# Hybrid encoder trunk: the attention heads run as one two-burst pipeline, and the projection's matmuls are ordered behind each burst

## Chip, cores, metric

One core of a Trainium2 chip. The metric is the device time of one execution in microseconds (us), median of three runs. PE is the matmul engine (TensorE; PEld its weight loads), DVE is VectorE, ACT is ScalarE, POOL is GpSimd, SP issues most DMAs.

## The reference, cut to what matters

Two layers; 512 tokens, width 2048. Per layer:

```python
h = rmsnorm(x, g_pre)
z = h @ w_in                      # one projection, columns split nine ways
log_a = log_sigmoid(ga @ w_alpha + b_alpha) / 16        # GLA decay
o_gla = rmsnorm(gla_chunk_causal(gq, gk, gv, log_a)) * silu(gg)   # 4 heads, state per 64-token chunk
o_att = rmsnorm(chunk_band_attention(aq, ak, av, rel_bias)) * silu(ag)  # 8 heads of 128
y = concat([o_gla, o_att]) @ w_out
x = x + rmsnorm(y, g_post)
```

For one attention head, with the 512 tokens in four tiles `i` of 128: scores of tile `i` against keys 0 to `(i+1)*128`, plus a bias by distance, softmax over the row, times `v`.

## The kernel before, in words

**The projections.** They are fp32-accurate products made of three reduced-format matmuls each: an operand is split into a high part (`wh`, an ACT cast, line 261) and a remainder (`wl`, a DVE subtraction, line 271). Blocks of weights are handled in pairs by a Strassen-like scheme: sums and differences of weight blocks (DVE, lines 255, 257, 278), seven products P1 to P7 with four chunks each. One "job" is one product and chunk. In the pair of query/key blocks (`feature_major`) a job is 24 matmuls of 128x256 (line 463); elsewhere it is 12 matmuls of 128x512 (line 473). Jobs come from one list, `stream`; loads, casts and remainders are made up to three jobs ahead. The buffers of `wh` come round every four jobs and those of `wl` every three, so a cast for a later job waits for the matmuls of an earlier one.

**The side work.** After each job, `pace()` calls `pump(n)`, which advances a generator in `tasks` by `n` steps (2.1 per job in the attention stretch). The generators trace the attention, the decay and the GLA heads in small pieces between the jobs.

**A head** (class `Head`) is made of these steps:

- `scores(i)` (lines 1044 to 1065): three matmuls into one PSUM tile; DVE adds the bias and takes the row extreme (line 1055, a custom operation and a read of its accumulator); ACT takes the exponential (line 1059).
- `trans(i)` (lines 1067 to 1076): the tile's probabilities are transposed on PE (line 1071) and copied out of PSUM by ACT (odd `i`, line 1074) or DVE (even `i`, line 1076).
- `mix(i)` (lines 1078 to 1095): probabilities times `v` on PE (line 1089, fp32: two passes each) into a quarter of one PSUM tile `ps_o`, kept for all four `i`; then ACT squares the quarter and sums it (line 1095, with a read of its accumulator).
- `gate()`: DVE adds up (line 1099), POOL takes the power -1/2 (line 524), DVE scales the four quarters (line 1103).
- `turn()`: four transposes of the gated output (line 1114), ACT out of PSUM (line 1117), a split, DMAs.

All these PSUM tiles come from one pool of four (`aux()`). A PE write into a tile waits until the earlier reads of the same tile are over, other columns included. This shows as waits in the order below.

**What sets the order.** The kernel is traced in program order; a list scheduler with a clock of its own then places each engine's instructions, by priority and readiness, and the engines run their lists strictly in that order. `tc.issue_after(x)` adds an edge: what is traced inside it goes behind `x` on the same engine's list. Before the change, two heads at a time are traced step by step by the string `ORDER`, one step per pump step, and nothing holds a job's matmuls back: the scheduler puts them wherever an attention step isn't ready.

Of the kernel before, what the change touches and what calls it, by code (L numbers as in the profile page):

```python
# [15 lines left out]
P = 128  # L16
L = 2
S = 512
# [18 lines left out]
def hybrid_trunk(  # L37
# [112 lines left out]
    lows, loads, last_turn, first_high = [], [], [None], []  # L150
    last_cast, last_low, last_mm, last_load, last_h, last_copy = [None], [None], [None], [None], [None], [None]
# [242 lines left out]
    def fast_gemm(l, pair, consume, rate=0.0, skip=0, feature_major=False, after=None, end=False, lag=0, ops=A, prod=None, acc=None, steps=False):  # L394
# [84 lines left out]
        def step(k, c):  # L479
            if k == "P2" and (end or gates) and c == 0 or k == "P5" and parted and c == 0 and "Z" not in acc:  # L480
                acc["Z"] = [aux()[:, :wide], aux()[:, :wide]]
            job = take(l, b0, k, c)
            behind = half_turns[1] if (k, c) == ("P4", 3) and half_turns else last_mm[0] if apart4 else None
            with tc.issue_after(behind) if behind else nullcontext():
                matmuls(job, k, c, range(2))
            issued.add((l, b0, k, c))
            ahead()
            if c == 3:
                if k == "P1" and not parted:
                    copies("p1", acc["X"])  # L490
                elif k == "P2" and parted:
                    copies("p2", acc[target[k]])
                elif k == "P5":
                    copies("p5", acc[target[k]])
                elif k == "P6":
                    copies("x", acc["X"])
                else:
                    if k == "P7" and (end or parted or gates):
                        copies("x7", acc["X"])
                    for t in range(2):  # L500
                        finished(k, t)
            if after is not None:
                after(k, c)
            pace()
# [340 lines left out]
    def layer(l):  # L845
# [42 lines left out]
        def forget_gate_decay():  # L888
# [6 lines left out]
            def finish_tile(t, la, lah, lal):  # L895
                if t % 2 == 0:
                    decay.append(slot(f"g{9 + t // 2}", [2, 512]))
                ps_d = aux()
                nc.tensor.matmul(ps_d, later, lah, start=True, stop=False)
                nc.tensor.matmul(ps_d, later, lal, start=False, stop=True)  # L900
# [6 lines left out]
            for t in range(NT):  # L907
                ps_g = aux()
# [9 lines left out]
                yield  # L918
                lah, lal = t2(dtype=F32R), t2(dtype=F32R)
                split(lah, lal, la)  # L920
                yield
                yield
                pend.append((t, la, lah, lal))
                if t:
                    finish_tile(*pend.pop(0))
                    yield
            for _ in range(4):
                yield
# [107 lines left out]
        class Head:  # L1036
# [7 lines left out]
            def scores(self, i):  # L1044
# [6 lines left out]
                nc.tensor.matmul(ps[:, :n], self.ql[:, t], self.kh[:, :n], start=False, stop=True)  # L1051
# [15 lines left out]
            def trans(self, i):  # L1067
                lk = (i + 1) * P
                ps = aux()
                for j in range(i + 1):  # L1070
                    nc.tensor.transpose(ps[:, j * P : (j + 1) * P], self.prob[i][:, j * P : (j + 1) * P], ident)  # L1071
                pt = self.pt[i] = t2((lk,))
                if i % 2:
                    nc.scalar.copy(pt, ps[:, :lk])
                else:
                    nc.vector.tensor_copy(pt, ps[:, :lk])

            def mix(self, i):
# [9 lines left out]
                for j in range(i + 1):  # L1088
                    nc.tensor.matmul(  # L1089
# [3 lines left out]
                    )  # L1093
# [33 lines left out]
        ORDER = (  # L1127
            "aS3 aS2 aS1 aS0 aT3 bS3 aT2 aP3 bS2 aT1 aP2 bS1 aT0 aP1 bS0 aP0 - aG "
            "bT3 bT2 bP3 bT1 bP2 bT0 bP1 bP0 - bG"
        ).split()  # L1130

        def attend(hd, qk):
            heads = {"a": Head(hd, qk, 0), "b": Head(hd + 1, qk, 1)}

            def turn(h):
                h.turn()
                if h.hd % 2:
                    heads_done.add(hd)

            for _ in range(5 if hd == HEADS[0] else 0):  # L1140
                yield
            for step in ORDER:
                if step == "-":
                    yield
                    continue
                h = heads[step[0]]
                if step[1] == "S":
                    h.scores(int(step[2]))
                elif step[1] == "T":
                    h.trans(int(step[2]))  # L1150
                elif step[1] == "P":
                    h.mix(int(step[2]))
                else:
                    h.gate()
                    delayed.append([8, lambda h=h: turn(h)])
                yield
# [4 lines left out]
        def qk_consume(p):  # L1161
            sets = {}

            def f(j, h, b, src, comb):
# [11 lines left out]
                if h and b:  # L1176
                    tasks.append(attend(4 * p + 2 * j, sets[j]))
# [7 lines left out]
        until(lambda: 0 in heads_done)  # L1185
        tasks.insert(0, forget_gate_decay())
# [482 lines left out]
```

## Time and profile before

| what | value |
|---|---|
| runs | 1583.02 us median of 3 (1581.57 to 1583.92) |
| the profiled execution's own time | 1582.65 us |
| its span, first to last instruction | 1580.5 us |
| PE busy | 1570.5 us, 99% |
| DVE busy | 1287.6 us, 81% |
| ACT busy | 928.6 us, 59% |
| attention stretch of layer 1 / layer 2 | about 236 to 490 us / 1024 to 1278 us |

The profiled execution lies 2.15 us over its span and 0.37 us under the median. Each row of a group in the profile gives the line, the engine, the operation, the tiles by name (`ax` is a PSUM tile of the side work, `mm` one of the projections), the shape, a count, and then the busy time, the mean ns of one, and the idle time before it with what ended that. In the timeline a row gives the start, the length from the first start to the last end, and the count of merged instructions.

### The profile page before, as it was taken

The numbers are of one execution on the slowest core, as the hardware profiler recorded it, in microseconds if no ns is written. First come the engines' busy times: TensorE is split into PE (matmuls) and PEld (weight loads), VectorE is DVE, ScalarE is ACT, GpSimd is POOL, SyncE is SP. The second block draws the span as 40 slices with busy tenths as digits, with TensorE's granted clock in tenths as the row PEclk, the third lists the DMA queues.
The fourth block names the chain that finished last, engine by engine and source line by source line (L and its number), as shares of the span: only waits on it lengthen the run. The fifth ranks groups of instructions, "written<-read, shape, count | busy, mean of one in ns | idle before, by whom it ended". The sixth has DMA issues, their size and how long they took to land.

```text
span 1580.5 us, 24991 instructions
## 1 busy us (share of the span) xinstructions
PE 1570.5 (99%) x9054; PEld 1363.2 (86%) x9054; DVE 1287.6 (81%) x1723; ACT 928.6 (59%) x1551; POOL 138.9 (9%) x230
## 2 busy tenths in 40 slices
PE   9999999999999999999999999999999999999998
PEld 7888999998888777888888899999988887788886
DVE  5989968578786978998989878785886878699887
ACT  7655545657555556665786446455674655576644
POOL 0221000001000000100122000001010000001001
PEclk9999999999999999999999999999999999999999
DMA  9888895785859768689879998847969597686987
GB/s 370 264 263 295 306 332 190 229 304 183 312 173 313 271 227 306 241 301 387 304 250 360 368 332 312 307 148 235 332 213 313 175 334 263 233 297 226 343 302 206
DMA packets 137738, 439.40 MB, mean 278 GB/s; under 512 B 15364, under 2 KB 27908, under 8 KB 137584
## 3 DMA queue, kind: packets, MB, share of 16 engines
q1 hardware_dynamic: 118800, 372.65, 67.3%
q0 software_dynamic: 18528, 64.88, 12.1%
q8 instruction: 71, 1.16, 0.3%
q14 instruction: 51, 0.42, 0.1%
q10 hardware_dynamic: 288, 0.30, 0.1%
HBM read 378.20 MB, written 61.62 MB: 278 GB/s over the span
## 4 chain that ended last, share of the span: by engine, by line
PE 94%; DMA 3%; DVE 1%; ACT 1%; issue 0%; POOL 0%; SPq 0%; POOLq 0%; DVEq 0%; ACTq 0%
PE mm L473 54%; PE mm L463 20%; PE ax L473 6%; PE mm L380 4%; PE ax L1089 2%; PE ax L1071 1%; PE ax L1278 1%; PE ax L1248 1%; DMA g<-in_w_ag_dram 1%; DMA A<-sa 1%; PE ax L1051 1%; PE ax L1049 1%; PE ax L1050 1%; DVE wl L271 1%; DMA sa<-S 0%
## 5 line engine op out<-in xcount | busy, mean ns | idle before, releaser
L473 PE MATMUL mm<-wh,sa 128*128 128x512 f32 (+1 forms) x1600 | 502.6, 387 | 0.8 <-DMA sa<-S 0.8
L473 PEld LDWEIGHTS mm<-wh,sa 128*128 128x128 f32 x1600 | 296.9, 188 | 61.6 <-DMA sa<-S 1.2
L261 ACT CAST wh<-raw 128x1024 fp32r<-128x1024 f32 (+2 forms) x233 | 234.3, 1009 | 191.3 <-PE mm L473 69.5
L271 DVE TENSOR_TENSOR wl<-raw,wh 128x1024 fp32r<-128x1024 f32 (+2 forms) x233 | 269.5, 1162 | 75.9 <-PE mm L473 33.7
L261 ACT CAST wh<-H 128x1024 fp32r<-128x1024 f32 (+1 forms) x208 | 211.9, 1021 | 177.9 <-PE mm L473 62.3
L473 PE MATMUL mm<-wl,sa 128*128 128x512 f32 (+1 forms) x800 | 310.1, 388 | 0.4 <-DVE wl L271 0.4
L271 DVE TENSOR_TENSOR wl<-H,wh 128x1024 fp32r<-128x1024 f32 (+1 forms) x208 | 245.0, 1179 | 47.4 <-PE mm L473 18.3
L463 PE MATMUL mm<-sa,wh 128*128 128x256 f32 x1280 | 236.1, 284 | 0.0
L473 PE MATMUL mm<-wh,a 128*128 128x512 f32 (+1 forms) x672 | 215.4, 387 | 0.0
L463 PEld LDWEIGHTS mm<-sa,wh 128*128 128x128 f32 x1280 | 199.8, 191 | 0.5
L463 PE MATMUL mm<-sa,wl 128*128 128x256 f32 x640 | 180.6, 284 | 0.0
L473 PEld LDWEIGHTS mm<-wl,sa 128*128 128x128 f32 x800 | 150.2, 188 | 30.9 <-DVE wl L271 1.6
L473 PEld LDWEIGHTS mm<-wh,a 128*128 128x128 f32 x672 | 124.4, 188 | 24.2
L255 DVE TENSOR_TENSOR H<-H,raw 128x1024 f32<-128x1024 f32 (+1 forms) x120 | 141.0, 1180 | 0.3
L473 PE MATMUL mm<-wl,a 128*128 128x512 f32 (+1 forms) x336 | 130.8, 390 | 0.5 <-DVE wl L271 0.5
L261 ACT CAST wh<-g 128x1024 fp32r<-128x1024 f32 x84 | 81.3, 974 | 76.3 <-DVE g L255 25.7
L463 PEld LDWEIGHTS mm<-sa,wl 128*128 128x128 f32 x640 | 122.1, 191 | 0.2
L473 PE MATMUL mm<-wh,g 128*128 128x512 f32 (+1 forms) x416 | 120.5, 367 | 0.0
L271 DVE TENSOR_TENSOR wl<-g,wh 128x1024 fp32r<-128x1024 f32 x84 | 93.7, 1119 | 16.3 <-PE mm L463 7.4
L463 PE MATMUL mm<-a,wh 128*128 128x256 f32 x512 | 94.9, 285 | 0.0
L524 POOL TENSOR_TENSOR sm<-sm,mhalf 128x2 f32<-128x2 f32 (+2 forms) x40 | 38.9, 973 | 615.7 <-DVE sm L1099 295.7
L421 ACT COPY ev<-mm 128x512 f32<-128x512 f32 (+1 forms) x112 | 64.2, 573 | 45.8 <-PE mm L473 31.2
(284 smaller groups left out, 2493.7 us busy)
## 6 DMA issues: line engine op xcount, KB each, us to landing
raw<-in_w_dram SPq DMA_DIRECT2D x287, 512.0 KB, 5.4
sa<-S SPq DMA_DIRECT2D x176, 512.0 KB, 4.4
sa<-A SPq DMA_DIRECT2D x48, 512.0 KB, 6.0
H<-in_w_dram SPq DMA_DIRECT2D x48, 512.0 KB, 5.1
sa<-oS SPq DMA_DIRECT2D x32, 512.0 KB, 5.8
g<-in_w_dram SPq DMA_DIRECT2D x20, 512.0 KB, 7.0
S<-g POOLq DMA_DIRECT2D x18, 512.0 KB, 7.9
raw<-in_w_ag_dram SPq DMA_DIRECT2D x32, 264.0 KB, 4.5
```

The costliest lines, as they stand in the source:

```text
L255: nc.vector.tensor_tensor(out=h, in0=h, in1=r, op=ALU.add)
L261: last_cast[0] = nc.scalar.copy(self.wh[:, z, :], src[:, z, :]).ins
L271: last_low[0] = nc.vector.tensor_tensor(out=self.wl[:, z, :], in0=self.src[:, z, :], in1=self.wh[:, z, :].bitcast(F32), op=ALU.subtract).ins
L380: nc.tensor.matmul(pss[o], a(part, kk, o) if callable(a) else a[:, part, t], rhs[:, kk, :], start=(i == 0 and kk == 0 and m == 0), stop=(i ...
L421: last_copy[0] = nc.scalar.copy(e, src[t]).ins
L463: nc.tensor.matmul(dst, lhs[:, kk, f], a[:, part, tok], start=(fresh and kk == 0 and m == 0 and ft % 2 == 0), stop=(c == 3 and kk == 1 and ...
L473: last_mm[0] = nc.tensor.matmul(out_ps[t], a[:, part, tok], rhs[:, kk, :], start=(fresh and kk == 0 and m == 0), stop=(c == 3 and kk == 1 ...
L524: nc.gpsimd.tensor_tensor(out=out_r, in0=v, in1=mhalf[:, : v.shape[-1]], op=ALU.pow)
L1049: nc.tensor.matmul(ps[:, :n], self.qh[:, t], self.kh[:, :n], start=True, stop=False)
L1050: nc.tensor.matmul(ps[:, :n], self.qh[:, t], self.kl[:, :n], start=False, stop=False)
L1051: nc.tensor.matmul(ps[:, :n], self.ql[:, t], self.kh[:, :n], start=False, stop=True)
L1089: nc.tensor.matmul(o, self.pt[i][:, j * P : (j + 1) * P], av[hd // 4, j // 2][:, j % 2, (hd % 4) * P : (hd % 4 + 1) * P], start=(j == 0), ...
```

## The change

1. `ORDER` and `attend` go. One generator, `attention()`, runs the eight heads as a pipeline. A head has four quarters: `first` (scores 3 and 2), `second` (transposes of 3 and 2, scores 1 and 0), `third` (mix 3 and 2, transposes of 1 and 0), `fourth` (mix 1 and 0, gate). Each burst traces a quarter of the older head and one of the next head together: `third` of the old with `first` of the new, then `fourth` of the old with `second` of the new. The turn of the head before that stands at the front of a burst. Between bursts it gives 5 to 7 pump steps to the jobs. After six heads the pipeline is emptied and the decay runs; then the last two heads.
2. Scores 1 and 0 now share one PSUM tile (`last_scores`: columns 0:256 and 256:512), as do the transposes of 1 and 0, which take one ACT copy in place of one ACT and one DVE copy.
3. `last_att` remembers the last matmul traced of the side work (scores, mix, the decay's second product). In the four pairs QK01, QK45, GK and GV0 each job's matmuls are traced inside `issue_after(last_att[0])`.
4. In `forget_gate_decay` the two products of tile `t-1` are traced right behind the gate product of tile `t`.

```diff
@@ fast_gemm.step
             behind = half_turns[1] if (k, c) == ("P4", 3) and half_turns else last_mm[0] if apart4 else None
+            if b0 in (QK01, QK45, GK, GV0) and last_att[0]:
+                behind = last_att[0]
             with tc.issue_after(behind) if behind else nullcontext():
                 matmuls(job, k, c, range(2))
...
@@ Head
-            def scores(self, i):
+            def scores(self, i, ps=None):
...
-                ps = aux()
+                ps = aux() if ps is None else ps
...
+            def last_scores(self):
+                ps = aux()
+                self.scores(1, ps[:, 0:256])
+                self.scores(0, ps[:, 256:512])
...
+        def attention():
...
+            def second(h):
+                h.trans(3)
+                h.trans(2)
+                h.last_scores()
+            def third(h):
+                h.mix(3)
+                h.mix(2)
+                h.trans(1, 0)
+            def fourth(h):
+                h.mix(1)
+                h.mix(0)
+                h.gate()
...
+            for z in (0, 1, 2, 3, 4, 5, None, "decay", 6, 7, None):
...
+                for n, old, new in ((7 if early else 5, third, first), (7 if early else 6, fourth, second)):
+                    if gated:
+                        turn(gated)
+                        gated = None
+                    if prev:
+                        old(prev)
+                    if h:
+                        new(h)
+                    for _ in range(n):
+                        yield
+                gated, prev = prev, h
```

The count of matmuls is the same before and after. What moves is the order. In the rows below `[waits ...]` names the engines' (or DMA queues') counters for which an instruction waits.

PE's list before, at the place where one head's mix(1) is done (`L1089`, output `ax_4087`, two matmuls; `L1071` is another tile's transpose, `L463` are the jobs' matmuls):

```order
L1071 MATMUL ax_4225<-cst,t_692_3986 128x128 [waits DVE_49]
L463 MATMUL mm_2935<-sa_4023,wh_4066 128x256 [waits DMAHW7_49]
L1089 MATMUL ax_4087<-g_263_1493,t_721_4137 128x128 [waits Activation_49]
L1089 MATMUL ax_4087<-g_263_1493,t_721_4137 128x128
L463 MATMUL mm_2935<-sa_4023,wh_4066 128x256
L463 MATMUL mm_2935<-sa_4023,wl_4120 128x256
L463 MATMUL mm_2935<-sa_4023,wh_4066 128x256 x2
L463 MATMUL mm_2935<-sa_4023,wl_4120 128x256
```

Behind mix(1) stand matmuls of jobs; mix(0) of this head, which writes the same PSUM tile, stands 29 rows further down.

PE's list after, in the burst of layer 1 that does `fourth` of the pipeline's second head and `second` of its third (`L1098` writes `ax_3251`: mix(1), then mix(0), of the older head; `L1080` the transposes of tiles 3 and 2, `L1051` to `L1053` with `ax_3411` scores 1 and then scores 0 of the newer head, `L464` the jobs):

```order
L464 MATMUL mm_2884<-sa_3163,wl_3225 128x256
L1098 MATMUL ax_3251<-g_175_980,t_548_3266 128x128 [waits Activation_49]
L1098 MATMUL ax_3251<-g_175_980,t_548_3266 128x128
L1080 MATMUL ax_3398<-cst,t_550_3275 128x128 [waits PE_49,Activation_49]
L1080 MATMUL ax_3398<-cst,t_550_3275 128x128 x3
L1080 MATMUL ax_3405<-cst,t_553_3283 128x128 [waits Activation_49]
L1080 MATMUL ax_3405<-cst,t_553_3283 128x128 x2
L1051 MATMUL ax_3411<-g_462_2806,g_460_2804 128x256 [waits DVE_49]
L1052 MATMUL ax_3411<-g_463_2807,g_460_2804 128x256
L1053 MATMUL ax_3411<-g_462_2806,g_461_2805 128x256
L1098 MATMUL ax_3251<-g_175_980,t_548_3266 128x128 [waits Activation_49]
L1051 MATMUL ax_3411<-g_462_2806,g_460_2804 128x256 [waits DVE_49]
```

Between mix(1) and mix(0) now stand only the seven transposes and scores 1; mix(0) waits for ACT; scores 0 stands directly behind mix(0) and waits for DVE; the next job's matmuls follow after scores 0.

DVE's list before, around one head's gate (`L1055` the reduction of a score tile, `L1099` the sum that starts the gate, `L1103` the gate's scaling, `L271` the jobs' remainders):

```order
L1055 ISA t_623_3606,sm_3607<-ax_3602,bias_2980 128x128 [waits PE_49]
L1055 ISA sm_3607 128x1
L1062 SCALAR_TENSOR_TENSOR sm_3610<-sm_3296 128x4 [waits Activation_49]
L271 TENSOR_TENSOR wl_3638<-raw_3286,wh_3592 128x1024 [waits PE_49]
L1025 MEMSET bias_3363 64x64 [waits Activation_49]
L1099 TENSOR_TENSOR sm_3683<-sm_3295,sm_3361 128x4 [waits DVE_49,Activation_49]
L271 TENSOR_TENSOR wl_3676<-raw_3594,wh_3641 128x1024 [waits PE_49]
L1103 SCALAR_TENSOR_TENSOR sg_3461<-ax_3460,sm_3684,sg_3461 128x128 [waits Pool_49]
L1103 SCALAR_TENSOR_TENSOR sg_3461<-ax_3460,sm_3684,sg_3461 128x128 x3
```

The head's own score tiles are reduced before `L1099`; no score tile is reduced between it and the scaling.

DVE's list after, at the same burst as the PE rows above (`L1083` copies the transposes of tile 2, `L1108` is the sum that starts the older head's gate, `L1057` reduces score tiles: `t_574` is scores 1 and `t_576` is scores 0 of the newer head, `L1112` the gate's scaling):

```order
L272 TENSOR_TENSOR wl_3376<-raw_3130,wh_3344 128x1024 [waits PE_49]
L1083 COPY t_572_3406<-ax_3405 128x384 [waits PE_49]
L1108 TENSOR_TENSOR sm_3390<-sm_2917,sm_3097 128x4 [waits Activation_49]
L1057 ISA t_574_3415,sm_3416<-ax_3411,bias_2770 128x256 [waits DVE_49,PE_49]
L1057 ISA sm_3416 128x1
L1112 SCALAR_TENSOR_TENSOR sg_3252<-ax_3251,sm_3391,sg_3252 128x128 [waits DMAHW2_49,Pool_49]
L1112 SCALAR_TENSOR_TENSOR sg_3252<-ax_3251,sm_3391,sg_3252 128x128 x3
L1057 ISA t_576_3422,sm_3423<-ax_3411,bias_2770 128x128 [waits DVE_49,PE_49]
L1057 ISA sm_3423 128x1
```

The gate's sum, which waits for ACT, now stands ahead of the reduction of scores 1. ACT's list there (`L262` the cast for a later job, `L1104` the squares of mix(1) and then of mix(0)):

```order
L1026 ACTIVATE bias_3099<-bias_3099 128x512 [waits DMAHW0_49]
L262 CAST wh_3379<-raw_3346 128x1024 [waits PE_49]
L1104 ACTIVATE t_565_3385,sm_2917<-ax_3251 128x128 [waits PE_49]
L1104 ACTIVATE t_566_3388,sm_2917<-ax_3251 128x128 [waits PE_49]
L1085 COPY t_570_3399<-ax_3398 128x512 [waits DMASW1_49,Activation_49]
L1061 ACTIVATE t_574_3415,sm_3238<-t_574_3415,sm_3416 128x256 [waits DVE_49,Activation_49]
```

Both squares stand behind that cast, which waits for PE.

More of the change, by code (lines that the diff above doesn't have):

```diff
@@ L899, in finish_tile @@
                 nc.tensor.matmul(ps_d, later, lah, start=True, stop=False)
-                nc.tensor.matmul(ps_d, later, lal, start=False, stop=True)
+                last_att[0] = nc.tensor.matmul(ps_d, later, lal, start=False, stop=True).ins
                 nc.scalar.activation(decay[t // 2][:, t % 2, :], ps_d, AF.Exp)
@@ L917, in forget_gate_decay @@
                 )
[L918 removed]
+                if t:
+                    finish_tile(*pend.pop(0))
                 lah, lal = t2(dtype=F32R), t2(dtype=F32R)
                 split(lah, lal, la)
[L921 to L922 removed]
                 pend.append((t, la, lah, lal))
[L924 to L925 removed]
+                for _ in range(4):
                     yield
[L927 to L928 removed]
+            yield
             finish_tile(*pend.pop(0))
@@ L1065, in scores, with trans @@
                     load_bias(HEADS.index(self.hd) + 2)
-            def trans(self, i):
-                lk = (i + 1) * P
+            def last_scores(self):
                 ps = aux()
[L1070 to L1074, printed above, removed]
+                self.scores(1, ps[:, 0:256])
+                self.scores(0, ps[:, 256:512])
+            def trans(self, *ix):
+                ps, n = aux(), sum(i + 1 for i in ix) * P
+                pt, o = t2((n,)), 0
+                for i in ix:
+                    self.pt[i] = pt[:, o : o + (i + 1) * P]
+                    for j in range(i + 1):
+                        nc.tensor.transpose(ps[:, o : o + P], self.prob[i][:, j * P : (j + 1) * P], ident)
+                        o += P
+                if 2 in ix:
+                    nc.vector.tensor_copy(pt, ps[:, :n])
                 else:
-                    nc.vector.tensor_copy(pt, ps[:, :lk])
+                    nc.scalar.copy(pt, ps[:, :n])
             def mix(self, i):
@@ L1125, in turn @@
                     nc.gpsimd.dma_start(oa_d[l][c], flat(z))
[L1127 to L1133, printed above, removed]
+        ready = []
+        def attention():
             def turn(h):
@@ L1137, in turn, with first @@
                 if h.hd % 2:
-                    heads_done.add(hd)
-            for _ in range(5 if hd == HEADS[0] else 0):
-                yield
-            for step in ORDER:
-                if step == "-":
-                    yield
[L1145 to L1156, printed above, removed]
+                    heads_done.add(h.hd - 1)
+            def first(h):
+                h.scores(3)
+                h.scores(2)
+            def second(h):
[10 more added lines that the diff above has]
+                h.gate()
+            for _ in range(5):
+                yield
+            prev = gated = None
+            for z in (0, 1, 2, 3, 4, 5, None, "decay", 6, 7, None):
+                if z == "decay":
+                    while 0 not in heads_done:
+                        yield
+                    yield from forget_gate_decay()
+                    continue
+                h = None
+                if z is not None:
+                    while z >= len(ready):
+                        yield
+                    h = Head(*ready[z])
+                early = z is not None and z < 4
+                for n, old, new in ((7 if early else 5, third, first), (7 if early else 6, fourth, second)):
[7 more added lines that the diff above has]
+                    for _ in range(n):
+                        yield
+                gated, prev = prev, h
+                if h is None:
+                    turn(gated)
+                    gated = None
+                    yield
         QKT = {(0, 1): ("g4", "g5", "g6", "g7"), (0, 0): ("g8", "g9", "g10", "g11"),
@@ L1176, in f @@
                 if h and b:
-                    tasks.append(attend(4 * p + 2 * j, sets[j]))
+                    if not ready:
+                        tasks.append(attention())
+                    ready.extend((4 * p + 2 * j + i, sets[j], i) for i in range(2))
             return f
```

10 lines of the change are left out of this document (5 added, 5 removed).

## The prediction

> **What bounds the kernel now.** I read the page first, then the busy time by window for the attention stretch, then PE's timeline inside it, and last the groups by form there, for what ACT and DVE need per step.
>
> ```profile
> span 1580.5 us, 24991 instructions
> PE 1570.5 (99%) x9054; PEld 1363.2 (86%) x9054; DVE 1287.6 (81%) x1723; ACT 928.6 (59%) x1551; POOL 138.9 (9%) x230
> ...
> PE 94%; DMA 3%; DVE 1%; ACT 1%; issue 0%; POOL 0%; SPq 0%; POOLq 0%; DVEq 0%; ACTq 0%
> ```
>
> PE is the bound: it is busy 99% of the span, and the chain that ended last is PE for 94%. A busy PE could still hide gaps, so the attention stretch by itself, in windows (first the window, then PE's busy time and count):
>
> ```profile
> 236.00:365.00 129.00, 129.00 (x1053) 127.49 (x1052) 97.23 (x169) 76.39 (x165) 7.95 (x11) 1.00 0.71 242
> 365.00:490.00 125.00, 125.00 (x621) 105.04 (x620) 95.90 (x130) 75.51 (x136) 11.48 (x16) 1.00 0.67 226
> ```
>
> PE has no idle time at all in these 254 us; DVE is busy 193.1 us and ACT 151.9 us of it. So no wait is there to be removed. A gain could only come from PE's own work, whose count of matmuls the change leaves alone, and any wait that the change adds to PE is paid in full.
>
> **Does a switch between jobs and attention cost PE anything?** PE's timeline before (start, length, count):
>
> ```profile
> 301.13 0.28 PE L463 MATMUL mm<-sa,wl 128*128 128x256 f32 x1
> 301.25 0.38 PE L1071 MATMUL ax<-cst,t 128*128 128x128 f32 x2
> 301.47 0.83 PE L1089 MATMUL ax<-g,t 128*128 128x128 f32 x6
> 302.06 0.48 PE L463 MATMUL mm<-sa,wh 128*128 128x256 f32 x2
> 302.38 0.28 PE L463 MATMUL mm<-sa,wl 128*128 128x256 f32 x1
> 302.50 0.40 PE L463 MATMUL mm<-sa,wh 128*128 128x256 f32 x2
> ...
> 326.28 0.27 PE L1071 MATMUL ax<-cst,t 128*128 128x128 f32 x1
> 326.31 0.48 PE L463 MATMUL mm<-sa,wh 128*128 128x256 f32 x2
> 326.62 0.28 PE L463 MATMUL mm<-sa,wl 128*128 128x256 f32 x1
> ```
>
> Starts tell the pitch, since lengths overlap: a job's matmul of 256 columns takes 0.12 (302.38 to 302.50). From 301.25 to 302.38 lie eight attention records and two job matmuls: 1.13 - 0.24 = 0.89, or 0.111 each. A single transpose between jobs takes 326.62 - 326.28 - 0.24 = 0.10. So a stretch of one costs no more per matmul than a stretch of eight: there is no price for entering. In the order, PE's attention and decay work stands in 162 stretches before and 64 after. Even 0.01 us for each of the 98 that go is 1.0 us; I take a gain of 0.5. The decay's joined products belong here: their inputs stand one job of 12 matmuls or more ahead in ACT's and DVE's lists, and I count nothing for them.
>
> **What the bursts add.** What goes on between a mix and the next one was hidden before. The same stretch on PE, on ACT and on DVE:
>
> ```profile
> 319.12 1.05 PE L1089 MATMUL ax<-g,t 128*128 128x128 f32 x8
> ...
> 322.52 0.38 PE L1071 MATMUL ax<-cst,t 128*128 128x128 f32 x2
> 322.74 0.83 PE L1089 MATMUL ax<-g,t 128*128 128x128 f32 x6
> ```
> ```profile
> 320.21 0.28 ACT L1095 ACTIVATE t<-ax 128x128 bf16<-128x128 f32 x1 [0.61 <-PE ax L1089]
> 320.38 0.19 ACT L1095 ACTIVATION_READ_ACCUMULATOR t<-ax 128x1 f32 x1
> 322.60 1.05 ACT L261 CAST wh<-raw 128x1024 fp32r<-128x1024 f32 x1 [2.02 <-PE mm L463]
> 323.56 0.63 ACT L118 ACTIVATE g<-ev 128x512 fp32r<-128x512 f32 x1
> ```
> ```profile
> 322.78 1.22 DVE L271 TENSOR_TENSOR wl<-raw,wh 128x1024 fp32r<-128x1024 f32 x1
> 323.92 1.22 DVE L278 TENSOR_TENSOR H<-H,raw 128x1024 f32<-128x1024 f32 x1
> 325.06 0.68 DVE L426 TENSOR_TENSOR ev<-mm,ev 128x512 f32<-128x512 f32 x1
> 325.66 0.68 DVE L119 SCALAR_TENSOR_TENSOR g<-ev,g 128x512 fp32r<-128x512 f32 x1
> ```
>
> Mix(3) ends at 320.17; its square runs on ACT from 320.21 to 320.57; mix(2), which writes the same PSUM tile, starts at 322.74, and the jobs' matmuls filled the time on PE. Here one also sees what always stands at such a place: when a job's last matmuls are out, ACT starts the cast for a later job (322.60, 0.08 after the stretch began) and is taken until the next instruction at 323.56; DVE starts the remainder at 322.78.
>
> In the changed order nothing of jobs stands between these steps. In the burst shown (fourth of one head with second of the next) PE does mix(1), seven transposes, scores 1, mix(0), scores 0, and only then the jobs. Mix(0) waits for mix(1)'s square. Scores 0 shares its tile with scores 1, so it waits until DVE has reduced scores 1; on DVE that reduction stands behind the gate's sum, and the sum waits for the square of mix(0), which PE issues directly before scores 0. So PE waits for a round trip through ACT and DVE that begins with its own last matmul. Its price, from the groups of the window 236 to 490 (mean ns behind the bar):
>
> ```profile
> L1076 DVE COPY t<-ax 128x384 f32<-128x384 f32 x8 | 4.4, 552 | 0.6 <-PE ax L1071 0.6
> ...
> L1055 DVE CUSTOM_DVE_ANT_0 t<-ax,bias 128x256 f32<-128x256 f32 x8 | 3.3, 417 | 0.0
> ...
> L1055 DVE DVE_READ_ACCUMULATOR2_ANT sm<- 128x1 f32 x32 | 2.6, 82 | 0.0
> ...
> L1099 DVE TENSOR_TENSOR sm<-sm,sm 128x4 f32<-128x4 f32 x8 | 1.3, 157 | 1.0 <-ACT t L1095 0.8
> ```
>
> Term 1, the round trip. Count from the burst's first matmul. Mix(1) is four records, 0.44; the transposes seven, 0.77; scores 1 three of 0.12; so mix(0) is due at 1.57 and scores 0 at 1.79. The cast holds ACT from 0.08 to 1.04, the square of mix(1) is over at 1.40: mix(0) isn't held when nothing else is queued. Its second pass starts at 1.68 and ends 0.27 later; then 0.04 to ACT, 0.36 for the square, 0.04 to DVE, 0.16 for the sum less some overlap, 0.50 for the reduction with its read, 0.05 back to PE. Scores 0 starts near 3.0: a wait of 1.2 us. Such bursts stand six times in each layer (the second quarters of heads 2 to 6 and of head 8 in the pipeline's order): 12 x 1.2 = 14.4 us.
>
> Term 2, what else is queued there. DVE passes of 1024 columns follow each other by 1.14 (322.78, 323.92), those of 512 columns by 0.60 (325.06, 325.66); an ACT pass of 512 columns holds ACT for 0.5 to 0.63 (323.56). The burst shown has only a remainder and the copy of tile 2's transposes, done in time: +0. In the others the order puts ahead of the reduction: two sums of weights, one of them between the gate's sum and the reduction (+1.7); a sum, two 512-column passes, and a third that waits for ACT's copy and cast behind the square (+2.4, and ACT has such a pass ahead of the squares); a sum, and ACT's turn of the bias ahead of the squares (+0.65); a sum and the same turn (+1.0); an eviction on ACT (+0.4). Together 6.15 a layer, 12.3 us.
>
> Term 3, the two bursts of a layer in which the pipeline starts. Mix(3) of the new head waits for its transposes' copy on ACT, behind the cast: 1.04 + 0.6 against 1.12, so 0.5; in the second start DVE also has two 512-column passes and a sum ahead of scores 1's reduction, 1.7 in all. 2.2 a layer, 4.4 us.
>
> Term 4, the mixes that follow their predecessor closely. Twice a layer mix(2) stands three transposes behind mix(3) and waits for its square behind a cast and the turn's 0.63, over at 2.03 against 1.63, 0.4 each. At the two ends of the pipeline mix(0) stands directly behind mix(1): the square is over at 1.9 (an eviction is queued too) or 1.40 against 0.44, so 1.5 and 1.0. One score waits 0.3 for its operand. 3.6 a layer, 7.2 us.
>
> Waits of scores 2 for the turn's eviction have 1.99 us of PE work as cover against at most 2.3, and I count them at nothing; if the cover fails it is 0.3 in each of six bursts. The copies that go (one of 128 columns on DVE per head) cost nothing on an engine with time left. The jobs' loads, casts and remainders are behind the waits too, but they are three jobs ahead, 8 us, and PE's waits give ACT and DVE time to catch up: nothing.
>
> Sum: 14.4 + 12.3 + 4.4 + 7.2 - 0.5 = 37.8 us. The profiled execution took 1582.65 (span 1580.5 and 2.15 around it; 0.37 below the median of 1583.02). So about 1620.
>
> **Rivals.** A, not slower: scores 0 and mix(0) don't really wait, because the counter that PE waits for is reached by an earlier instruction of ACT and DVE than I take it for. Then the tied bursts run through, terms 1 to 4 go, and the time is 1582.65 - 0.5 = 1582; a whole 0.04 us for each stretch saved would give 1579. It holds if the waits end at least 1.2 us sooner than worked out in all 12 bursts. For it: PE had no wait in 254 us. Against: the square, the sum and the reduction are 0.36, 0.16 and 0.50 us long, and nothing stands between mix(0) and scores 0 to cover them.
>
> B, only the round trips: ACT and DVE are so far ahead, through the waits themselves, that nothing else is queued in them. Then term 2 goes and terms 3 and 4 halve: 14.4 + 5.8 - 0.5 gives 1602.
>
> C, the clock. Twice a layer the wait for scores 0 comes to about 2.9 to 3.6 us of idle PE. The first matmuls of the program, after idle time, were slow:
>
> ```profile
> L807 PE MATMUL ax<-t 128*128 128x512 bf16 x10 | 4.0, 586 | 1.2 <-DVE t L804 1.2
> ```
>
> Ten in 4.0 us is 0.40 each, against 0.24 for 512 columns at the jobs' pitch: 1.6 us lost in ten. If an idle time of this length brings that back, four times, it adds 6.4: 1626. [...]
>
> D, worse queues: DVE's sums in the bursts wait for weights that come late, or the remainders fall behind and PE waits for `wl` after the bursts too. Term 2 doubled and 0.3 in each of twelve bursts gives 1636.
>
> **How the numbers follow.** My forecast, terms 1 to 4 within a third: 0.53. B 0.17, D 0.14, C 0.07, A 0.09. The likeliest is 1620. The range reaches from B's 1602, less 2 for the unknown entry, to D's 1636 and 6 for C on top of it: 1600 to 1642, and A and the tails are left out. What a measurement can tell from no change here is about 0.2%, 3.2 us. Faster by more needs A with the dear entries: 0.03. Within it, the rest of A: 0.06. Slower: 0.91.
>
> **What would show it.** Right: PE idle in the attention stretch where it had none, in the list of waits as scores (line 1051) for DVE's reduction (line 1057), some twelve or more times of 1.2 us and up, and mix (line 1098) for ACT's square (line 1104); DVE's and ACT's busy times as before; job pitch 0.12 and the time outside the attention unchanged. Wrong: PE busy through the bursts, or waits of PE for `wl` instead, or a job pitch that has changed.

## The result, and the profile after

The changed kernel takes 1638.15 us (median of 6 runs, 1636.95 to 1639.79), the kernel before 1582.3 us (6 runs): a ratio of 1.0355, with an interval of 1.0341 to 1.0368. The profiled execution took 1639.79 us with a span of 1638.0.

The head of the page of the changed kernel, with the shares of the chain that ended last:

```profile
span 1638.0 us, 24922 instructions
...
PE 1590.6 (97%) x9054; PEld 1374.6 (84%) x9054; DVE 1289.7 (79%) x1707; ACT 932.7 (57%) x1551; POOL 136.8 (8%) x230
...
PE 88%; DVE 5%; ACT 2%; issue 2%; DMA 2%; SPq 0%; POOL 0%; POOLq 0%; DVEq 0%; ACTq 0%
```

DVE and ACT do what they did (1287.6 and 928.6 us before). PE is idle for 1638.0 - 1590.6 = 47.4 us where it was idle for 10.0, and busy 20.1 us longer with the same 9054 matmuls. So of the 57.5 us of span, 37.4 are idle time, and 20.1 lie in rows that count as busy, of the same matmuls. The two windows of the attention stretch (window, PE's busy time and count, the other engines', the granted clock behind POOL):

```profile
236.00:365.00 129.00, 119.88 (x951) 117.39 (x950) 83.68 (x140) 66.10 (x136) 6.86 (x8) 0.97 0.63 212
365.00:490.00 125.00, 118.65 (x601) 99.94 (x600) 93.82 (x125) 72.59 (x131) 9.21 (x15) 0.99 0.67 228
```

Where PE had no idle time it now has 254.0 - 238.53 = 15.5 us, and the granted clock, 1.00 before, is 0.97 and 0.99. Whom PE waits for, over the whole span (us in total, times, longest):

```profile
PE ax L1051 <- DVE sm L1057: 25.2, 14, 3.0
PE ax L1098 <- ACT t L1104: 8.8, 16, 1.4
PE mm L474 <- DVE wl L272: 2.2, 4, 0.6
PE ax L1098 <- ACT t L1085: 1.9, 4, 0.5
PE ax L1052 <- DVE g L110: 1.3, 4, 0.5
```

Scores (line 1051) wait 14 times for DVE's reduction (1057), mixes (1098) 16 times for ACT's square (1104). Without the products' wait for a remainder (line 474) the attention's waits are 37.2 us in 38 pieces: the new idle time. One of the longest, on PE, ACT and DVE:

```profile
271.40 0.28 PE L1053 MATMUL ax<-g,g 128*128 128x256 f32 x1
271.66 0.49 PE L1098 MATMUL ax<-g,t 128*128 128x128 f32 x2
275.16 0.39 PE L1051 MATMUL ax<-g,g 128*128 128x256 f32 x1 [3.01 <-DVE sm L1057]
275.38 0.28 PE L1052 MATMUL ax<-g,g 128*128 128x256 f32 x1
```
```profile
272.18 0.28 ACT L1104 ACTIVATE t<-ax 128x128 bf16<-128x128 f32 x1 [0.58 <-PE ax L1098]
272.36 0.19 ACT L1104 ACTIVATION_READ_ACCUMULATOR t<-ax 128x1 f32 x1
```
```profile
271.42 1.23 DVE L256 TENSOR_TENSOR H<-H,raw 128x1024 f32<-128x1024 f32 x1
272.56 0.55 DVE L1083 COPY t<-ax 128x384 f32<-128x384 f32 x1
273.02 0.15 DVE L1108 TENSOR_TENSOR sm<-sm,sm 128x4 f32<-128x4 f32 x1
273.54 1.23 DVE L258 TENSOR_TENSOR raw<-H,raw 128x1024 f32<-128x1024 f32 x1 [0.36 <-DMA raw<-in_w_dram]
274.68 0.42 DVE L1057 CUSTOM_DVE_ANT_0 t<-ax,bias 128x256 f32<-128x256 f32 x1
```

Scores 1 is out at 271.40, mix(0) at 271.66, its square at 272.55. But the reduction of scores 1 runs only at 274.68: what DVE's list has ahead of it runs first in these rows, a sum for a later job, a copy, the gate's sum and one more sum for a later job, which itself waits 0.36 us for weights that had not landed.

What such a wait costs beyond its idle time is seen in the same rows. The second matmul of mix(0) starts 0.49 - 0.28 = 0.21 behind the first, at 271.87, and scores 0 was due 0.11 later, at 271.98; it started at 275.16, 3.18 late, where the row counts 3.01 from the modelled end. And its second pass follows 0.22 behind the first (275.38 - 275.16), where 0.12 is the pitch. So 0.17 + 0.10 = 0.27 us come on top of this wait. The other waits of the attention in the first layer show 0.16 to 0.17, and at full clock 0.10, in the same way; for all 38 I estimate 38 x 0.27 = 10.3 us.

The rest is the clock. Windows of 3.41 us in the changed kernel, three pairs (PE's busy time first, the granted clock third from the end):

```profile
272.47:275.89 3.42, 0.73 (x6) 0.73 (x7) 3.06 (x10) 1.16 (x4) 1.04 (x1) 1.00 0.12 48
275.89:279.30 3.41, 3.41 (x18) 3.41 (x18) 0.62 (x4) 0.50 (x2) 0.00 (x0) 0.50 0.30 82
330.50:333.91 3.41, 0.63 (x5) 0.63 (x6) 2.82 (x9) 1.93 (x6) 1.41 (x1) 1.00 0.90 316
333.91:337.32 3.41, 3.41 (x18) 3.41 (x18) 1.40 (x7) 0.50 (x3) 0.00 (x0) 0.50 0.62 196
398.76:402.17 3.41, 1.96 (x12) 1.54 (x10) 2.26 (x2) 2.39 (x5) 0.00 (x0) 1.00 0.36 136
402.17:405.58 3.41, 3.41 (x16) 2.87 (x17) 1.32 (x6) 0.55 (x3) 1.03 (x1) 1.00 0.00 0
```

In 275.89 to 279.30 PE runs at half clock with no wait at all: 18 job matmuls where 3.41 / 0.12 = 28 fit. Six such stretches lie in the attention of the changed kernel, three a layer, none in that of the kernel before.

### The profile page after: what moved, and what is told of

It reads as the page before. It is cut to its first block, busy times and chain, and to the rows that moved or that the text cites. A ratio compares the mean times of both kernels' runs of the same rounds, so it can differ in the third digit from the quotient of the medians.

```text
span 1638.0 us, 24922 instructions
## 1 busy us (share of the span) xinstructions
PE 1590.6 (97%) x9054; PEld 1374.6 (84%) x9054; DVE 1289.7 (79%) x1707; ACT 932.7 (57%) x1551; POOL 136.8 (8%) x230
## 3 DMA queue, kind: packets, MB, share of 16 engines
q8 instruction: 71, 1.16, 0.3%
## 4 chain that ended last, share of the span: by engine, by line
PE 88%; DVE 5%; ACT 2%; issue 2%; DMA 2%; SPq 0%; POOL 0%; POOLq 0%; DVEq 0%; ACTq 0%
PE mm L474 52%; PE mm L464 18%; PE ax L474 6%; PE mm L381 4%; DVE wl L272 2%; PE ax L1098 1%; PE ax L1314 1%; PE ax L1284 1%; ACT wh L262 1%; PE ax L1051 1%; DVE H L256 1%; PE ax L1052 1%; DMA raw<-in_w_dram 1%; PE ax L1053 1%; DMA raw<-in_w_ag_dram 0%
## 5 line engine op out<-in xcount | busy, mean ns | idle before, releaser
L262 ACT CAST wh<-raw 128x1024 fp32r<-128x1024 f32 (+2 forms) x233 | 234.3, 1009 | 189.0 <-PE mm L474 66.9
L262 ACT CAST wh<-H 128x1024 fp32r<-128x1024 f32 (+1 forms) x208 | 212.1, 1021 | 201.2 <-PE mm L474 85.1
L464 PE MATMUL mm<-sa,wh 128*128 128x256 f32 x1280 | 238.4, 288 | 0.0
L464 PEld LDWEIGHTS mm<-sa,wh 128*128 128x128 f32 x1280 | 204.7, 196 | 0.0
L464 PE MATMUL mm<-sa,wl 128*128 128x256 f32 x640 | 183.2, 288 | 0.0
L262 ACT CAST wh<-g 128x1024 fp32r<-128x1024 f32 x84 | 81.3, 975 | 78.4 <-DVE g L256 26.8
L464 PEld LDWEIGHTS mm<-sa,wl 128*128 128x128 f32 x640 | 125.3, 196 | 0.0
L464 PE MATMUL mm<-a,wh 128*128 128x256 f32 x512 | 92.9, 283 | 0.0
```

The lines of the kernel that those rows point to most:

```text
L262: last_cast[0] = nc.scalar.copy(self.wh[:, z, :], src[:, z, :]).ins
L464: nc.tensor.matmul(dst, lhs[:, kk, f], a[:, part, tok], start=(fresh and kk == 0 and m == 0 and ft % 2 == 0), stop=(c == 3 and kk == 1 and ...
```

## The experiments

The tie is the third point of the change: in the four pairs a job's matmuls may not run before the last attention matmul of the burst. My theory after the result: tied bursts cost what they make PE wait for, and PE waits because within a burst a matmul writes into a PSUM tile that ACT or DVE must first read; the half clock is a second price of the same waits. The rivals: the tie itself (products are held back, so that ACT and DVE fall behind and PE waits wherever it next needs them), the pipeline and the joined copies, and the joined decay products.

| kernel | median us | ratio to before | interval |
|---|---|---|---|
| changed | 1638.15 | 1.0355 | 1.0341 to 1.0368 |
| without the tie | 1581.44 | 0.9992 | 0.9983 to 1.0001 |
| before, with the tie alone | 1598.31 | 1.0111 | 1.0095 to 1.0126 |
| scores 0 and 1 in own tiles | 1608.61 | 1.0166 | 1.0152 to 1.0180 |
| scores' readers behind | 1601.68 | 1.0124 | 1.0109 to 1.0139 |
| all readers behind | 1585.51 | 1.0022 | 1.0012 to 1.0032 |
| all readers behind, no tie | 1582.01 | 0.9999 | 0.9991 to 1.0008 |
| gate last | 1628.88 | 1.0296 | 1.0282 to 1.0310 |
| short sums | 1627.94 | 1.0291 | 1.0276 to 1.0307 |
| short sums, gate last | 1618.44 | 1.0229 | 1.0212 to 1.0247 |
| waits filled | 1632.96 | 1.0318 | 1.0304 to 1.0333 |
| decay as before | 1640.13 | 1.0367 | 1.0353 to 1.0381 |

### Without the tie

```diff
-            if b0 in (QK01, QK45, GK, GV0) and last_att[0]:
-                behind = last_att[0]
```

> The changed kernel without the tie: products are no longer queued behind the last attention matmul of a burst, the pipeline over eight heads, the joined copies and the decay's order stay. Theory (PE waits in the bursts because nothing else may run there): products fill the bursts again, PE's waits in the attention fall from 37 us to under 3, no half-clock stretch is left, 1580 to 1588. Rival (the pipeline's order, the joined copies or the shared tile cost time by themselves): still over 1600, with PE waits at the scores and mixes.

1581.44 us, as the theory had it. PE's share on the page is that of the kernel before:

```profile
span 1581.7 us, 24919 instructions
...
PE 1571.4 (99%) x9054; PEld 1363.5 (86%) x9054; DVE 1283.7 (81%) x1707; ACT 930.0 (59%) x1551; POOL 141.0 (9%) x230
```

The pipeline over eight heads, the joined copies and the shared tile cost nothing by themselves (and bring nothing). All of the loss needs the tie. Whether by the holding back itself or by the waits in the bursts, this run does not say.

### The readers behind both writers

Three edits of one kind, all with tie, bursts and shared tiles kept. Scores 1 and scores 0 are both issued before the first reduction; mix(3) and mix(2) before their squares, mix(1) and mix(0) before theirs:

```diff
                 self.scores(1, ps[:, 0:256])
                 self.scores(0, ps[:, 256:512])
+                self.soft(1)
+                self.soft(0)
...
                 h.mix(1)
                 h.mix(0)
+                h.square(1)
+                h.square(0)
```

(soft and square are the reduction with its exponential, and the square, taken out of scores and mix.)

> The changed kernel with each reader of a shared PSUM tile issued behind both of its writers: scores 1, scores 0, then both reductions; mix(3), mix(2), then both squares; mix(1), mix(0), then both squares. Tiles, tie and bursts stay. Theory: nearly all waits in the bursts go; what is left are the starts of the pipeline (a mix that waits for the copy of its transposes, a score for its operand, about 5 us in all): 1582 to 1590, no half-clock stretch. If grouping itself saves PE 0.04 us a stretch, 1579. Rival (the tie lets ACT and DVE fall behind): over 1615, with waits at other lines.

1585.51 us, within the theory's range. The tie is in place and the loss is gone but for 3.2 us, so the tie does not make ACT and DVE fall behind in these bursts. The same two windows as above, and what is left of waits in the attention:

```profile
236.00:365.00 129.00, 128.41 (x1050) 126.69 (x1049) 95.04 (x153) 74.39 (x156) 8.97 (x10) 1.00 0.71 240
365.00:490.00 125.00, 125.00 (x618) 105.11 (x617) 95.12 (x130) 76.23 (x142) 10.58 (x16) 1.00 0.66 226
```
```profile
PE ax L1105 <- ACT t L1092: 1.0, 2, 0.5
PE ax L1053 <- DVE g L110: 0.9, 2, 0.5
```

1.9 us in four waits at the pipeline's starts. PE's busy time is 1571.1 us in this run, against 1570.5 before: that the work now lies in long bursts saves PE nothing that can be seen.

Then the scores' part alone (the first two added lines of the diff, the squares left in mix):

> The changed kernel with scores 1 and scores 0 both issued ahead of the two reductions (shared tile kept); the squares stay between the mixes. Theory: all waits of scores 0 go (about 27 us) and the half clock with them (about 9 us), the waits of mix for the squares stay (12 to 14 us), no tile is missing: 1597 to 1603; what is left against the kernel with all readers behind (1585.5) is the price of the squares' places. Rival (a wait that goes comes back at the next step of the burst): over 1608.

1601.68 us, within the theory's range. Waits of scores for the reduction no longer stand in the list; the squares' do:

```profile
PE ax L1105 <- ACT t L1111: 10.7, 8, 1.9
PE ax L1105 <- ACT t L1092: 1.7, 2, 0.8
```

One half-clock stretch is left, from 1176.16, behind a window of 3.41 us in which PE was idle for 54%. So the order of scores and reductions is worth 1638.15 - 1601.68 = 36.5 us, that of mixes and squares the other 16.2. And all three edits with the tie's two lines removed:

> The changed kernel with each reader of a shared tile issued behind both of its writers, and without the tie. Theory (PE is the bound and the order of its work is worth nothing once it doesn't wait): 1580 to 1583, within 0.2% of the kernel before. Rival (the one pipeline with joined copies brings something when nothing waits): under 1578.

1582.01 us, a ratio of 0.9999 (0.9991 to 1.0008): none of the versions of this order that were run beats the kernel before.

### Scores 0 in a tile of its own

```diff
-                ps = aux()
-                self.scores(1, ps[:, 0:256])
-                self.scores(0, ps[:, 256:512])
+                self.scores(1)
+                self.scores(0)
```

> The changed kernel with scores 1 and scores 0 in PSUM tiles of their own; tie and bursts stay. Theory (scores 0 waits for DVE to read its neighbour in the shared tile): the waits of scores 0 go (27.6 us of lost pitch, 25.2 us of idle PE) and with them the half-clock stretches (about 9 us); the waits of mix(0) for ACT's square stay; a burst then needs one tile more, so a wait of up to 0.3 us in each of 12 bursts may come instead: 1600 to 1606. Rival (the tie lets ACT and DVE fall behind, and PE waits wherever it next needs them): the time stays within 10 us of 1638, with waits of the same sum at other lines, the products' remainders among them.

1608.61 us, 2.6 above the theory's range. PE's waits:

```profile
PE ax L1097 <- ACT t L1103: 8.8, 16, 1.4
PE ax L1051 <- ACT t L1084: 5.6, 6, 0.9
PE ax L1051 <- DVE t L1082: 1.4, 2, 0.7
```

Of the 25.2 us for the reduction none is left, so it was the shared tile. In its place come 7.0 us in 8 waits for the copy of the transposes, up to 0.9 each instead of my 0.3. The burst now needs a fifth tile from a pool of four, which fits these waits; a larger pool was not run. The squares' 8.8 us stand as they did.

### What holds the reduction: the gate's sum, or DVE's list

The prediction let the wait of scores 0 run through mix(0), its square and the gate's sum (term 1), and put DVE's and ACT's other work on top (term 2). First the gate is issued behind the new head's scores, so that the reduction stands ahead of the gate's sum:

```diff
                 h.mix(1)
                 h.mix(0)
-                h.gate()
...
                     if h:
                         new(h)
+                    if prev and old is fourth:
+                        prev.gate()
```

> The changed kernel with the gate of the old head issued behind the scores of the new one, so that on DVE the reduction of scores 1 stands ahead of the gate's sum; the shared tiles, tie and bursts stay. Theory (scores 0 waits for a round trip that runs through mix(0), its square and the gate's sum): the trip then is only scores 1 and its own reduction, 0.1 to 0.5 us behind mix(0) instead of 1.2 and up; the sums of weights that stood between the gate's sum and the reduction are passed too. PE's waits for the reduction fall from 25.2 us to 6 to 11, most half-clock stretches go: 1606 to 1620. Rival (the shared tile alone sets the wait, the gate's sum is no part of it): over 1630.

1628.88 us: between the theory's range and the rival's, and both miss. The waits for the reduction fall by 7.8 us and not by 14 to 19:

```profile
PE ax L1051 <- DVE sm L1057: 17.4, 12, 2.2
PE ax L1098 <- ACT t L1104: 9.5, 16, 1.4
```

DVE in one of the bursts where nothing was won, in the run with the gate last (scores 1 is out at 372.02 there):

```profile
371.57 1.21 DVE L272 TENSOR_TENSOR wl<-H,wh 128x1024 fp32r<-128x1024 f32 x1
...
372.82 1.23 DVE L256 TENSOR_TENSOR H<-H,raw 128x1024 f32<-128x1024 f32 x1
373.96 0.55 DVE L1083 COPY t<-ax 128x384 f32<-128x384 f32 x1
374.43 0.41 DVE L1057 CUSTOM_DVE_ANT_0 t<-ax,bias 128x256 f32<-128x256 f32 x1
```

No gate's sum is there, and the reduction still comes 2.4 us behind its scores: a remainder and a sum of 1024 columns, work for jobs that come later, are ahead of it. So I cut the sums of weights to 64 columns in the pairs concerned:

```diff
+                z = slice(0, 32 if self.b0 in (QK01, QK45, GK) else None)
...
-                        nc.vector.tensor_tensor(out=h, in0=h, in1=r, op=ALU.add)
+                        nc.vector.tensor_tensor(out=h[:, :, z], in0=h[:, :, z], in1=r[:, :, z], op=ALU.add)
```

> The changed kernel with DVE's sums of weights cut from 1024 to 64 columns in the jobs of the pairs QK01, QK45 and GK (so the sums are left out nearly whole, and the products use unsummed weights); order, bursts, tie, tiles stay nearly as they are. Theory (in half of the bursts it is DVE's sums queued ahead of the reduction that end last, not the round trip through mix(0)): the waits of scores 0 fall from 3.2, 1.2, 3.0, 1.3, 2.0, 1.2 us in a layer to about 1.2 each, 1.9 where 512-column passes stand ahead, some 4 us less a layer, and half or more of the half-clock stretches go: 1621 to 1629. Rival (the round trip sets the waits alone): 1635 to 1640.

> The same cut of the sums, and the gate of the old head behind the scores of the new one. Theory (round trip and queue are two ways to the same wait, the later one counts, and only both edits together take it away): the waits of scores 0 fall to some 3 us a layer from 11.8, hardly a half-clock stretch is left: 1607 to 1615, further below the changed kernel than the two edits' gains apart would say only by the clock. Rival (a third thing holds the reduction): over 1622.

1627.94 and 1618.44 us. Short sums alone fall into the theory's range; both edits together miss it by 3.4 us, though not as far as the rival's. How late scores 0 starts in the six bursts of the first layer (its start less the due start, worked out from PE's timeline as above), and what the prediction took for the whole burst. The prediction counted from the burst's first matmul, so its figure also holds what mix(0) is late; that is 0.40, 0.40, 0.52 and 0.54 us in the last four bursts of the changed kernel, the same within 0.01 in the other three, and stands beside the changed kernel's figure:

| burst (changed kernel, us) | predicted | changed | gate last | short sums | both |
|---|---|---|---|---|---|
| 272 | 2.9 | 3.18 | 1.53 | 2.52 | 2.26 |
| 302 | 1.2 | 1.21 | 0.57 | 1.21 | 0.57 |
| 330 | 3.6 | 3.01 (+0.40) | 2.33 | 2.01 | 1.34 |
| 356 | 1.85 | 1.28 (+0.40) | 1.20 | 1.24 | 0.36 |
| 381 | 2.2 | 2.00 (+0.52) | 1.93 | 1.16 | 0.43 |
| 497 | 1.6 | 1.16 (+0.54) | under 0.25 | 1.16 | under 0.25 |

At 302 and 497 the round trip through the gate's sum is the wait; at 356 it and the list end nearly together, so that each edit alone wins under 0.1 and both win 0.9; at 381 the list ends last, and behind it waits the round trip of 1.16. The two are not a sum but a race of which the later one counts. At 330 only the list is seen: in the changed kernel the gate's sum starts there 1.30 us after the square is over (332.13 against 330.83) and waits for nothing. What the edits take out of one list does add up: 0.68 with the gate last, which also moves the split of an operand behind the reduction, and 1.00 with short sums are 1.67 with both. The burst at 272 is a third thing, in the run with both edits:

```profile
269.97 0.23 DVE L257 TENSOR_TENSOR H<-H,raw 128x64 f32<-128x64 f32 x1
271.50 0.23 DVE L259 TENSOR_TENSOR raw<-H,raw 128x64 f32<-128x64 f32 x1 [1.31 <-DMA raw<-in_w_dram]
271.64 0.55 DVE L1085 COPY t<-ax 128x384 f32<-128x384 f32 x1
272.11 0.41 DVE L1059 CUSTOM_DVE_ANT_0 t<-ax,bias 128x256 f32<-128x256 f32 x1
```

A sum cut to 0.23 us waits 1.31 us for weights to land, and the reduction behind it waits with it.

### The clock by itself

In the three bursts of a layer that a half-clock stretch follows, idle matmuls are put in, in two of them between mix(0) and scores 0, in the third between scores 1 and mix(3). They write a tile that nobody reads:

```diff
+                fill = {3: 10, 1: 10, 4: 6}.get(self.hd, 0)
...
+                            behind = nc.tensor.matmul(z, self.qh[:, 0:P], self.kh, start=True, stop=True).ins
```

> The changed kernel with idle matmuls of 128x512 between mix(0) and scores 0 in the three bursts of a layer that a half-clock stretch follows (ten in two of them, six in the third; they write a tile that nobody reads). They fill the wait and should not lengthen it. Theory that the half clock follows an idle PE and has a price of its own: the six stretches go and the time falls by 8 to 10 us, 1628 to 1630, at unchanged waits. Rival (the half clock costs nothing beside the waits, or comes from something else): 1636 to 1642.

All six stretches are gone in the profiled execution. In the changed kernel and then in the filled one, the same 4 us of products behind the burst:

```profile
275.50:279.50 4.00, 4.00 (x24) 4.00 (x23) 1.01 (x6) 0.80 (x4) 0.00 (x0) 0.57 0.26 70
```
```profile
275.50:279.50 4.00, 4.00 (x36) 4.00 (x35) 1.55 (x4) 1.55 (x3) 0.00 (x0) 1.00 0.37 92
```

36 matmuls instead of 24, at a pitch of 0.12: a stretch costs 12 x 0.12 = 1.44 us, six cost 8.6. The spans of the two profiled runs differ by 1638.0 - 1629.9 = 8.1. The medians differ by 5.2, and 1632.96 lies between the theory's range and the rival's. Two things account for it, by estimate. A stretch is 3.41 x 0.5 / 1638 = 0.001 of the granted clock; that is 0.993 to 0.995 in the six runs of the changed kernel (0.9935 on average) and 0.997 to 0.999 in the four of the filled one (0.9983), so the edit takes away some 4.6 stretches a run and not six: 6.6 us. And the filler did lengthen the bursts: its tile too is a fifth from the pool, it waits 0.9 us for one in four bursts, and scores 0 comes 0.32 and 0.52 us later behind the start of the bursts at 272 and 330, less the 0.10 that a wait costs its second pass, some 1.3 us in two layers. 6.6 - 1.3 = 5.3 us is near the 5.2 measured.

### The tie on the old order, and the decay

The kernel before, with the tie's two lines and its bookkeeping (last_att is set at the last matmul of each score and mix and of the decay's product) and nothing else of the change:

```diff
+            if b0 in (QK01, QK45, GK, GV0) and last_att[0]:
+                behind = last_att[0]
```

> The kernel before with nothing but the tie added (a product that comes up for the four pairs is queued behind the last attention or decay matmul issued so far); its order by two heads, its tiles and copies stay. Theory (the tie costs only where a tied stretch holds two steps of which one waits for the reader of the other): the stretches of the old order are mostly one or two independent steps, so PE waits little, 1585 to 1598. Rival (the tie costs by itself, since ACT and DVE fall behind the products that are held): 1615 and more.

1598.31 us, 0.3 above the theory's range; the tie is not free without bursts either. PE's waits in it:

```profile
PE ax L1052 <- DVE sm L1058: 5.1, 2, 2.5
PE ax L1053 <- DVE g L110: 4.6, 2, 2.3
```

Two places a layer: a score that waits until DVE has reduced an earlier one, and a score whose operand DVE has not split yet. PE has only tied products behind such a score: what used to run while a score waited may not, as in the bursts. The tie alone costs 16 us here. In the profiled execution, 14.6 us longer than that of the kernel before (1595.1 - 1580.5), these four waits are 9.7 us; two half-clock stretches follow them (from 424.09 and 1219.39, behind windows idle for 73 and 75%), by the price above 2.9 us, and 0.27 us on top of each wait makes 1.1. The rest, about 1 us, was not traced.

And the changed kernel with the decay's steps as they were before:

```diff
-                if t:
-                    finish_tile(*pend.pop(0))
+                yield
                 lah, lal = t2(dtype=F32R), t2(dtype=F32R)
                 split(lah, lal, la)
+                yield
+                yield
                 pend.append((t, la, lah, lal))
+                if t:
+                    finish_tile(*pend.pop(0))
```

> The changed kernel with the decay's products in the order of the kernel before (not joined). Theory (joining them costs and brings nothing, their inputs are ready a job ahead): 1636 to 1640. Rival (the joined products wait for the split of their input): 1630 to 1634.

1640.13 us, 0.1 above the theory's range, a ratio of 1.0367 (1.0353 to 1.0381) beside 1.0355 (1.0341 to 1.0368) for the changed kernel: the decay's joined products neither cost nor bring anything that can be told.

## Why the prediction was right, and where its sum was short

The forecast was 1620 with a range of 1600 to 1642; the time is 1638.15. The direction and the mechanism were right, the sum of 37.8 us was too small by 18. That the range held this is in part luck: its upper end was D's 1636 and 6 for C on top, and D's reason did not come true.

- **The bound.** Right: PE is the bound, and waits put into it are paid in full (37.4 us more idle time, 57.5 us more span). Without waits the same order runs in 1582.01.
- **No price for entering a stretch, nothing for the decay.** Right: PE's busy time with bursts and no waits is 1571.1 against 1570.5, and the decay's order moves nothing that can be told. The 0.5 us of gain can't be seen.
- **Terms 1 and 2, scores 0.** Expected 13.35 us a layer in six bursts. Measured: scores 0 is 3.18 + 1.21 + 3.01 + 1.28 + 2.00 + 1.16 = 11.84 late, and mix(0) ahead of it 0.40 + 0.40 + 0.52 + 0.54 = 1.86, together 13.7. Each burst is within 0.35 of its figure. The size was right, the working only half: I took 1.2 us of round trip everywhere and added the lists to it. With the gate moved only 7.8 us of PE's idle time went, not 14.4. In the bursts at 272, 330 and 381 the gate's sum waits for nothing, DVE reaches it late; there the 1.2 stands for time that the list takes by itself. And at 272 part of it is a sum that waits for its weights, which I had under rival D.
- **Term 3, the starts.** Mix(3) and scores 0 start 0.58, 0.71 and 1.95 late: 3.24 a layer against 2.2.
- **Term 4, close mixes.** 0.53, 0.54, 1.61 and 1.12, and 0.63 and 0.37 for the operands of two scores, of which I had one: 4.8 a layer against 3.6.
- **What a wait costs besides.** That a single matmul between others costs no more holds where PE runs on (0.10 for a transpose alone, 0.111 in a row of eight records); behind a wait the second pass comes 0.10 late. 38 times, 3.8 us, not in the sum.
- **Rival C, the clock.** I gave it 0.07 and 6.4 us, as an alternative; it came on top, six times and not four, with 8.6 us. I tied it to one idle time of 2.9 to 3.6 us; in the changed kernel it also came behind 0.71 and 1.95 us in one window (below).

So terms 1 to 4 came to 2 x (13.7 + 3.24 + 4.8) = 43.5 us instead of 38.3, within the third that I allowed them. The 5.2 they lack, 3.8 for second passes, 8.6 of half clock and the 0.5 of gain that isn't there make the 18 us. The step that was wrong is that the clock was priced as an alternative to the sum and not as a term of it.

By the profile's own account: 37.2 us of idle time, 10.3 for what each wait costs beyond it, 8.6 of half clock: 56.1 of the 57.5 us that the span grew. The 1.4 left were not traced; the products' waits for remainders (2.2 us in the list) are among the candidates.

Rivals A and B fall with the list of waits. D's 1636 is nearest in number, but its reason isn't: remainders late behind the bursts are 2.2 us in all.

## What to carry to other kernels

Before work is gathered into a burst that nothing else may enter, look in it for a matmul that writes a tile which another engine reads within the same burst; issue all writers of such a tile before the first reader: here the bursts then ran through (1585.5 us instead of 1638.2). A reader's delay was here not its own length (0.50 us for the reduction of scores 1 with its read) but everything that its engine's list had ahead of it at that moment (scores 0 3.18 us late at 272), sums whose weights hadn't landed included (a wait of 0.36 us there). And where PE loses no time at each switch (0.10 us for a transpose alone, 0.111 a record in a row of eight), nothing was won by gathering: the same order without the tie and the waits is at 0.9999 of the kernel before (0.9991 to 1.0008).

## What the runs showed of the hardware

In the changed kernel each of the six half-clock stretches in the attention lasts 3.41 us, and their starts lie a whole number of such lengths apart (275.89 and 333.91: 58.02 us, 17 x 3.413). With its span counted from these starts in windows of that length, up to the one that starts at 1627.57, PE was idle for 60 to 82% of the six windows ahead of a stretch, and for 42% at most of each of the others. PE was busy for 0.73 and 0.63 us of the windows ahead of the two stretches above, and for 1.96 us of the one at 398.76, which none followed. Closer together, in the run with the gate last:

```profile
324.94:328.35 3.41, 1.73 (x14) 1.73 (x15) 2.53 (x8) 1.91 (x6) 0.00 (x0) 1.00 0.86 302
328.35:331.76 3.41, 3.41 (x31) 3.41 (x30) 2.07 (x7) 1.14 (x3) 1.03 (x1) 1.00 0.73 213
372.72:376.14 3.42, 1.66 (x9) 1.34 (x10) 2.43 (x8) 1.63 (x6) 0.00 (x0) 1.00 0.24 89
376.14:379.55 3.41, 3.41 (x10) 2.67 (x9) 1.36 (x6) 0.31 (x2) 1.03 (x1) 0.50 0.50 151
```

Idle for 49% of the window: full clock after it. Idle for 51%: half. These shares go by the ends of matmuls as the profile models them. With the short sums full clock followed a window idle for 56% (at 268.82, busy for 1.51 of 3.41 us), so no share at which it turns was shown. In the changed kernel the wait of 2.00 us at 381 is cut in two by a border of these windows at 381.70 (PE idle for 28% of the one before it, 36% of the one after) and full clock followed both, while 0.71 and 1.95 us fall nearly wholly into one window (470.44 to 473.86, idle for 62%), and half clock followed. Two of the seven windows at half clock in the attention of the run with the gate last follow another one, of which PE was busy for 2.78 and 2.80 us. The first of them:

```profile
1137.31:1140.72 3.41, 2.78 (x13) 2.78 (x14) 1.72 (x8) 1.09 (x4) 0.42 (x1) 0.50 0.75 237
1140.72:1144.14 3.42, 3.42 (x18) 3.42 (x18) 1.16 (x5) 0.19 (x1) 0.61 (x1) 0.50 0.48 139
```

Busy for 2.78 of 3.41 us at half clock: half clock again. In the changed kernel PE was idle for 0 to 7% of each of the six windows at half clock, and full clock followed every one.
